# w_down of a mixture of experts loaded in longer runs of memory, with its inner index permuted

## Chip, core and metric

The kernel runs on one core of a Trainium2 chip. The metric is the device time of one execution in microseconds (us). The core has TensorE (PE, with its weight loads shown apart as PEld), VectorE (DVE), ScalarE (ACT), GpSimd (POOL), SyncE (SP, which here only issues DMAs), and 16 DMA engines that move data between HBM and SBUF.

## What is computed

One layer of a flow-matching backbone for one sample: 512 latent tokens of width 1024 and 256 context tokens. A mixer (Fourier branch, recurrent branch, merge gates, output projection) comes first; then a feed-forward part with 16 experts, in which each expert picks its 64 best tokens; then a final RMSNorm. The change lies in the experts:

```python
def expert_choice_ffn(h, w_router, w_gate, w_up, w_down):
    cap = CAPACITY_FACTOR * T // N_EXPERTS                      # 64
    scores = jax.nn.softmax(jnp.einsum('btd,de->bte', h, w_router), axis=-1)
    g, idx = lax.top_k(jnp.swapaxes(scores, 1, 2), cap)
    xg = jax.vmap(lambda hb, ib: hb[ib])(h, idx)
    hid = jax.nn.silu(jnp.einsum('becd,edf->becf', xg, w_gate)) * jnp.einsum('becd,edf->becf', xg, w_up)
    out = jnp.einsum('becf,efd->becd', hid, w_down) * g[..., None]
    return jax.vmap(lambda ib, ob: jnp.zeros((T, D), h.dtype).at[ib.reshape(-1)].add(ob.reshape(-1, D)))(idx, out)
```

All weights are float32 and each is used once. Per expert, w_gate and w_up are 1024 × 1536 and w_down is 1536 × 1024: 3 × 6.29 MB, 18.87 MB.

## The kernel before

**Stages.** The mixer takes the first part of the run. Its weights come in tiles of 1024 rows × 256 columns, so in pieces of 1 KB (`load_next`, L190 and L202); among them w_ada, whose rows are 24 KB long and of which a partition takes eight neighbouring rows, and w_in, with rows of 18 KB. Then come routing and 16 experts, then the tail: the last expert's w_down by parts of the width, and the norm.

**One expert** (the loop over `e`, up to L1216). `up_gate` multiplies the 64 gathered tokens (`xg`, in the trace `g`) with w_gate into `G`, then with w_up into `U`: eight tiles each, 32 matmuls of 384 columns each (L1111). The inner width of 1536 is held in two halves f of 768 = `FH` columns: half f lies on PSUM partitions 64 f to 64 f + 63, so `sl`, SiLU(G) × U, is 128 partitions × 768 columns. Six transposes (L1193) turn blocks of 128 of these columns into `T`, and ACT copies them (L1194) to `hT`, two tiles of three blocks, in the trace `wa` and `wd`. The w_down matmuls (L1206) take `hT` as stationary and w_down as moving operand, into `Y`; the two halves dh of the width of 1024 go to the upper and the lower 64 partitions, side by side on the array. Hooks between the tiles put in the scatter of the expert before (L1127), the ranking two experts ahead, and, in every odd expert, the gather for the next two (L1083, ahead of the transposes). On float32 a matmul leaves two records, a transpose one.

**Weight stream.** `eload` issues one tile of 768 KB per call on SP's queue: 24 units per expert in the order gate, up, down, into a ring of 22 places (rings of 14, 5 and 1 in `ew`, and `wd` and `we`). Each use of a tile is followed by one `eload`, so the stream runs about 22 tiles ahead of PE at most. Gate and up tiles (L856) are 128 whole rows of 6 KB, one per partition: one block of memory. Each DMA takes the next of eight semaphores in turn, whichever engine issues it, and before it is issued the queue waits for the DMA that used that semaphore before; so eight are under way at most.

Two small transfers on ACT's queue take places in that turn: at e = 2 `g20` is filled from `g2` (in the trace `we<-g`, L1185), and at e = 14 `g2` is copied within itself (`g<-g`, L1212). The first one stands on ACT behind the SiLU of expert 2 (L1167).

**w_down before.** A unit of experts 0 to 14 is one half dh of the width (512 columns, 2 KB) of 3 × 128 rows (L854): partition p holds rows p, p + 128 and p + 256 of them, three pieces of 2 KB. Two units, dh = 0 and 1, serve three steps of the inner width. The last expert's w_down has units of its own (`LAST`), of 512 and then 256 columns.

Of the kernel before, what the change touches and what calls it, by code (L numbers as in the profile page):

```python
# [17 lines left out]
P = 128  # L18
D = 1024
KD = D // P  # L20
# [7 lines left out]
NE = 16  # L28
CAP = 64
DE = 1536  # L30
FH = DE // 2
# [45 lines left out]
def layer(ctx: ExitStack, tc: tile.TileContext, I, out):  # L77
    nc = tc.nc
# [16 lines left out]

    # ------------------------------------------------------------------ long-lived tiles
    keep, close_keep = open_pool("keep")
# [18 lines left out]
    ident = cst[:, 0:128]  # L116
# [28 lines left out]

    # ------------------------------------------------------------------ weight stream of the mixer
    w_in, w_ada = I["w_in"][0], I["w_ada"][0]
# [151 lines left out]

    # ------------------------------------------------------------------ start: tokens, constants, adaLN of layer input  # L300
    st_p, close_st = sb("st", "right")
# [129 lines left out]

    # ------------------------------------------------------------------ constants of the recurrence
    c2, c4n, hba, hbi = (lru_c[:, i, :] for i in (4, 5, 6, 7))
# [24 lines left out]

    # ------------------------------------------------------------------ Fourier columns, as the modulation arrives
    zF = [zt("zF0"), zt("zF1")]  # L460
# [82 lines left out]

    # ------------------------------------------------------------------ 2-D DFT of the Fourier group, by its symmetries
    fT = bt.tile([P, 10, 258], F32R, tag="bt", name="fT")
# [71 lines left out]
    load_next()  # L617
    # ------------------------------------------------------------------ Fourier map to the model width
    def y4_mm(o, w, f, j, last):
# [26 lines left out]

    # ------------------------------------------------------------------ recurrent branch
    lr, close_lr = sb("lr", "right")
# [92 lines left out]

    # ------------------------------------------------------------------ merge gate A
    def zcols(w, o, c, tick=None):
# [17 lines left out]
    for i in range(4):  # L761
# [14 lines left out]
        ada_acc(J_A + i)  # L776
    # ------------------------------------------------------------------ GeLU gate times recurrence
    gp, close_gp = sb("gp", "right")
    gH = gp.tile([P, H, T], F32R, name="gH")
    gL = gp.tile([P, H, T], F32R, name="gL")  # L780
    for i in range(4):
# [10 lines left out]
        ada_acc(J_G + i)  # L792
    # ------------------------------------------------------------------ merge gate B with the recurrent map
    mH = []
# [26 lines left out]
    close_hl()  # L821
    # ------------------------------------------------------------------ expert weight stream
    NR = (14, 5, 1)
# [7 lines left out]
    EW = {}  # L831
# [3 lines left out]
    def eload():  # L835
        n = ring["n"]
        if n >= len(units):
            return
        ring["n"] += 1
        e, wn, q = units[n]  # L840
        m, i = n % (sum(NR) + 2), 0
        while i < 3 and m >= NR[i]:
            m, i = m - NR[i], i + 1
        t = rings[i].tile([P, DE], F32, tag="ew", bufs=NR[i], name=f"ew{n}") if i < 3 else held[m]
        if e == NE:
            t = t[:, 0:D]
            nc.sync.dma_start(t, flat(I["final_g"], 0, [[0, P], [1, D]]))
            EW["fg"] = t
            return
        src = I[wn][0, e]  # L850
        if wn == "w_down_e":
            c0, cw, k0, nk = q if e == NE - 1 else (512 * (q % 2), 512, 3 * (q // 2), 3)
            t = t[:, 0:cw * nk].rearrange("p (k d) -> p k d", k=nk)
            nc.sync.dma_start(t, src[P * k0:P * (k0 + nk), c0:c0 + cw].rearrange("(k p) d -> p k d", p=P))  # L854
        else:
            nc.sync.dma_start(t, src[P * q:P * q + P, :])  # L856
        EW[e, wn, q] = t

    # ------------------------------------------------------------------ output projection, residual, routing
    rt, close_rt = sb("rt", "right")  # L860
# [145 lines left out]

    # ------------------------------------------------------------------ experts
    mps, close_mps = open_pool("mps", space=PSUM)
# [146 lines left out]
    for e in range(NE):  # L1155
# [33 lines left out]
        for a in range(2):  # L1189
            t = at("T", (P, 3, P))  # L1190
            for b in range(3):
                j = 3 * a + b
                pe.transpose(t[:, b, :], sl[:, P * j:P * j + P], ident)  # L1193
            act.copy(hT[a], t)  # L1194
# [4 lines left out]
        yp = at("Y")  # L1199
        for r in range(4):  # L1200
            w = [EW.pop((e, "w_down_e", 2 * r + dh)) for dh in range(2)]
            for i in range(3):
                kf = 3 * r + i
                f, j = divmod(kf, 6)
                for dh in range(2):
                    pe.matmul(yp[64 * dh:64 * dh + 64, :], hT[j // 3][:, j % 3, 64 * f:64 * f + 64], w[dh][:, i, :],  # L1206
                              start=kf == 0, stop=kf == 11, tile_position=(0, 64 * dh))
            eload()
            eload()
# [7 lines left out]

    # ------------------------------------------------------------------ last expert by halves of the width, final norm
    ov = out[0].rearrange("(n p) d -> p n d", p=P)
# [116 lines left out]
```

## Time and profile before

| | |
|---|---|
| median of three runs | 1219.57 us (1216.5 to 1226.09) |
| span of the profiled execution | 1215.1 us |
| PE busy | 1145.7 us, 94% |
| DVE, ACT, POOL busy | 46%, 24%, 9% |
| DMA | 368.01 MB, 303 GB/s over the span |

The span runs from the first to the last instruction of one profiled execution. A page divides it into 40 slices of 30.4 us each; the digits of a slice are the busy share in tenths, and the GB/s line tells what the DMA engines moved in it. PE's busy time is not PE at its peak, since matmuls overlap. A line such as "Y<-ew,wa" names the tile written and those read.

### The profile page before, as it was taken

The page shows a single profiled execution, that of the slowest core. Times are in us where ns is not written, and L with a number is a line of the kernel's source. Part 1 is how long each engine was busy: PE and PEld are TensorE (multiplying, and loading weights), DVE is VectorE, ACT ScalarE, POOL GpSimd, SP SyncE. Part 2 cuts the span into 40 slices and gives each one's busy share as a digit, 9 for nine tenths or more (in the row PEclk, how much of TensorE's full clock was granted, in tenths as well). Part 3 has the DMA queues.
Part 4 walks back from the last instruction along what each step waited for, and adds up shares of the span by engine and source line. Part 5 has one row for each costly group of instructions (what it writes and reads, how often), then busy time and mean ns, then how long its engine had stood idle before and what let it go on. Part 6 is the DMA issues. An engine that isn't in the chain of part 4 may idle for free. (4 is left out here: it accounts for less than half of the span.)

```text
span 1215.1 us, 16698 instructions
## 1 busy us (share of the span) xinstructions
PE 1145.7 (94%) x6873; PEld 684.3 (56%) x6891; DVE 564.3 (46%) x1053; ACT 286.2 (24%) x448; POOL 112.7 (9%) x118
## 2 busy tenths in 40 slices
PE   8989988899999999999999999999999899999886
PEld 4768766688888897545445454344344344344333
DVE  5556899987666665232332342232232232232024
ACT  5543777634322222101001001001001001001004
POOL 4254343210000000000000000000000000000002
PEclk9989988999999999999999999999999999999999
DMA  8912011154664595999999999999999999999996
GB/s 310 318 62 91 21 45 53 49 183 150 207 199 148 181 395 213 314 387 416 364 408 417 403 407 418 403 408 419 409 410 418 413 413 414 410 414 411 404 399 212
DMA packets 146155, 368.01 MB, mean 303 GB/s; under 512 B 8912, under 2 KB 61656, under 8 KB 145952
## 3 DMA queue, kind: packets, MB, share of 16 engines
q1 hardware_dynamic: 143408, 363.52, 78.1%
q0 software_dynamic: 1088, 2.18, 0.6%
q10 hardware_dynamic: 1584, 1.25, 0.4%
q8 instruction: 54, 0.88, 0.3%
q14 instruction: 21, 0.17, 0.0%
HBM read 364.43 MB, written 2.10 MB: 302 GB/s over the span
## 5 line engine op out<-in xcount | busy, mean ns | idle before, releaser
L1111 PE MATMUL U<-ew,g 128*64 128x384 f32 x928 | 168.6, 495 | 10.4 <-DMA ew<-in_w_up_e 10.0
L1111 PE MATMUL G<-ew,g 128*64 128x384 f32 x960 | 174.5, 493 | 2.1 <-DMA ew<-in_w_gate_e 1.6
L1130 DVE TENSOR_TENSOR x<-x,sc 128x512 f32<-128x512 f32 x120 | 77.1, 684 | 101.9 <-PE sc L1127 101.9
L1111 PEld LDWEIGHTS U<-ew,g 128*64 128x64 f32 x928 | 59.6, 136 | 93.9 <-issue 55.0
L1111 PEld LDWEIGHTS G<-ew,g 128*64 128x64 f32 x960 | 65.7, 136 | 81.2 <-issue 60.2
L1244 POOL TENSOR_TENSOR o<-x,ew 128x512 f32<-128x512 f32 (+1 forms) x8 | 7.8, 1004 | 938.2 <-ACT o L1240 938.2
L1206 PE MATMUL Y<-ew,wd 128*64 128x512 f32 x324 | 82.8, 595 | 5.6 <-DMA ew<-in_w_down_e 5.5
L1210 DVE SCALAR_TENSOR_TENSOR wc<-Y,gc,g 128x512 f32<-128x512 f32 x15 | 11.3, 751 | 160.5 <-PE Y L1206 160.5
L1206 PE MATMUL Y<-ew,wa 128*64 128x512 f32 x312 | 78.1, 599 | 7.8 <-DMA ew<-in_w_down_e 4.6
L1194 ACT COPY wa<-T 128x384 f32<-128x384 f32 x16 | 7.7, 479 | 255.4 <-PE T L1193 255.4
L230 DVE TENSOR_TENSOR wL<-raw,wH 128x1024 fp32r<-128x1024 f32 x48 | 62.9, 1340 | 2.0 <-ACT wH L229 1.6
L1206 PEld LDWEIGHTS Y<-ew,wd 128*64 128x64 f32 x324 | 24.3, 137 | 56.5 <-issue 41.5
L1167 ACT ACTIVATE wc<-G 128x768 f32<-128x768 f32 x16 | 13.0, 811 | 178.8 <-PE G L1111 178.8
L1083 PEld LDWEIGHTS xg<-wa,xn 128*128 128x128 f32 x448 | 51.1, 192 | 0.2
L1083 PE MATMUL xg<-wa,xn 128*128 128x128 f32 x448 | 51.2, 275 | 0.0
L1206 PEld LDWEIGHTS Y<-ew,wa 128*64 128x64 f32 x312 | 23.5, 136 | 48.6 <-issue 31.7
L1049 DVE TENSOR_SCALAR wc<-wa,score 128x128 bf16<-128x128 f32 (+3 forms) x63 | 23.9, 379 | 57.0 <-ACT wa L1042 57.0
L1213 ACT CAST wb<-wc 128x512 fp32r<-128x512 f32 x15 | 9.3, 617 | 169.3 <-DVE wc L1210 169.3
L674 PE MATMUL ga<-u,gw 128*128 128x512 f32 x64 | 36.0, 645 | 10.0 <-issue 9.9
L1127 PEld LDWEIGHTS sc<-wb 64*128 64x128 f32 x240 | 23.9, 184 | 35.9 <-issue 35.3
L229 ACT CAST wH<-raw 128x1024 fp32r<-128x1024 f32 x38 | 38.0, 1045 | 18.3 <-PE zO L426 9.9
L699 POOL TENSOR_TENSOR th<-tp,th 128x768 f32<-128x768 f32 x16 | 35.0, 2205 | 49.2 <-DVE tp L698 49.2
(360 smaller groups left out, 2191.2 us busy)
## 6 DMA issues: line engine op xcount, KB each, us to landing
ew<-in_w_gate_e SPq DMA_DIRECT2D x120, 768.0 KB, 13.3
ew<-in_w_up_e SPq DMA_DIRECT2D x116, 768.0 KB, 15.0
ew<-in_w_down_e SPq DMA_DIRECT2D x113, 768.0 KB, 15.0
raw<-in_w_ada SPq DMA_DIRECT2D x24, 1024.0 KB, 5.5
raw<-in_w_in SPq DMA_DIRECT2D x16, 1024.0 KB, 4.8
wd<-in_w_down_e SPq DMA_DIRECT2D x7, 768.0 KB, 12.5
we<-in_w_down_e SPq DMA_DIRECT2D x7, 768.0 KB, 12.9
wd<-in_w_up_e SPq DMA_DIRECT2D x6, 768.0 KB, 14.6
```

The source lines that it names most:

```text
L229: (copy or act.copy)(wH[:, a], raw[:, a])
L230: dve.tensor_sub(wL[:, a], raw[:, a], wH[:, a].bitcast(F32))
L674: pe.matmul(gf[:, 512:1024], gw[:, d, i, :], u[:, TC:TA], start=True, stop=True)
L699: pool.tensor_tensor(b, s, b, op=OP.mult)
L1049: dve.tensor_scalar(GT[c][:, 0:m], sB[:, 0:m], s, None, op0=OP.is_lt)
L1083: pe.matmul(a[k // 4][:, P * (k % 4) + q.start:P * (k % 4) + q.stop], XN[n // 2][:, n % 2, P * k:P * k + P], oh[:, n, q], start=n == 0, st ...
L1111: pe.matmul(t[64 * f:64 * f + 64, n, 0:384], xg[:, k, c:c + CAP], w[:, o:o + 384], start=k == 0, stop=k == KD - 1, tile_position=(0, 64 * f))
L1127: pe.matmul(a[dh][:, c], w, v, start=j == 0, stop=j == 1, tile_position=(64 * dh, 0))
L1130: dve.tensor_add(xs, xs, a[dh])
L1167: act.activation(v3(sl), G[:, :, 0:384], AF.Silu)
L1206: pe.matmul(yp[64 * dh:64 * dh + 64, :], hT[j // 3][:, j % 3, 64 * f:64 * f + 64], w[dh][:, i, :], start=kf == 0, stop=kf == 11, tile_posi ...
L1210: dve.scalar_tensor_tensor(y, yp, gc[:, e % 3:e % 3 + 1], g2, op0=OP.mult, op1=OP.mult)
```

## The change

w_down of experts 0 to 14 is taken in pieces of 6 KB. Within each half f of the inner width, partition p now holds the six neighbouring rows 6 p to 6 p + 5, 24 KB in a row in memory; a unit is a quarter of that, 6 KB per partition, so one and a half rows of w_down. Block j of the inner width is then made of the rows 6 p + j instead of 128 j + p, and so the transposes read every sixth column of `sl`. A unit holds the whole width for one and a half blocks; the matmuls of a unit are three (j, dh) in the order of memory. The last expert keeps the sizes of its units, with the permuted rows.

```diff
         if wn == "w_down_e":
-            c0, cw, k0, nk = q if e == NE - 1 else (512 * (q % 2), 512, 3 * (q // 2), 3)
-            t = t[:, 0:cw * nk].rearrange("p (k d) -> p k d", k=nk)
-            nc.sync.dma_start(t, src[P * k0:P * (k0 + nk), c0:c0 + cw].rearrange("(k p) d -> p k d", p=P))
+            if e == NE - 1:
+                c0, cw, k0, nk = q
+                f, j = divmod(k0, 6)
+                t = t[:, 0:cw * nk].rearrange("p (k d) -> p k d", k=nk)
+                nc.sync.dma_start(t, src[FH * f:FH * f + FH, c0:c0 + cw].rearrange("(p k) d -> p k d", k=6)[:, j:j + nk])
+            else:
+                f, j = divmod(q, 4)
+                nc.sync.dma_start(t, src[FH * f:FH * f + FH, :].rearrange("(p k) d -> p (k d)", k=6)[:, DE * j:DE * j + DE])
...
                 j = 3 * a + b
-                pe.transpose(t[:, b, :], sl[:, P * j:P * j + P], ident)
+                pe.transpose(t[:, b, :], sl[:, j:FH:6], ident)
...
         yp = at("Y")
-        for r in range(4):
-            w = [EW.pop((e, "w_down_e", 2 * r + dh)) for dh in range(2)]
+        for q in range(KD):
+            w = EW.pop((e, "w_down_e", q))
+            f = q // 4
             for i in range(3):
-                kf = 3 * r + i
-                f, j = divmod(kf, 6)
-                for dh in range(2):
-                    pe.matmul(yp[64 * dh:64 * dh + 64, :], hT[j // 3][:, j % 3, 64 * f:64 * f + 64], w[dh][:, i, :],
-                              start=kf == 0, stop=kf == 11, tile_position=(0, 64 * dh))
-            eload()
+                j, dh = divmod(3 * (q % 4) + i, 2)
+                pe.matmul(yp[64 * dh:64 * dh + 64, :], hT[j // 3][:, j % 3, 64 * f:64 * f + 64], w[:, 512 * i:512 * i + 512],
+                          start=f == 0 and j == 0, stop=f == 1 and j == 5, tile_position=(0, 64 * dh))
             eload()
```

In the program of before, PE comes to the w_down matmuls of expert 0 so (the DMAHW semaphores are those of the loads, the Activation one that of the copies to `hT`):

```order
L1206 MATMUL Y<-ew_3738,wa 64x512 [waits DMAHW2_49,Activation_49]
L1206 MATMUL Y<-ew_3740,wa 64x512 [waits DMAHW3_49]
L1206 MATMUL Y<-ew_3738,wa 64x512
L1206 MATMUL Y<-ew_3740,wa 64x512
L1206 MATMUL Y<-ew_3738,wa 64x512
L1206 MATMUL Y<-ew_3740,wa 64x512
L1206 MATMUL Y<-ew_3742,wd 64x512 [waits DMAHW4_49,Activation_49]
L1206 MATMUL Y<-ew_3748,wd 64x512 [waits DMAHW5_49]
```

and in the changed program, at the same place:

```order
L1210 MATMUL Y<-ew_3738,wa 64x512 [waits DMAHW2_49,Activation_49]
L1210 MATMUL Y<-ew_3738,wa 64x512 x2
L1210 MATMUL Y<-ew_3740,wa 64x512 [waits DMAHW3_49]
L1210 MATMUL Y<-ew_3740,wa 64x512 x2
L1210 MATMUL Y<-ew_3742,wd 64x512 [waits DMAHW4_49,Activation_49]
L1210 MATMUL Y<-ew_3742,wd 64x512 x2
L1210 MATMUL Y<-ew_3748,wd 64x512 [waits DMAHW5_49]
```

The first six matmuls used two tiles in turn; now three use one tile, then three the next, and the wait for the second tile has moved two matmuls down.

On SP's queue the end of an expert's up loads and the w_down loads behind them stood so in the program of before (expert 1):

```order
L856 DMA ew_4119<-in_w_up_e 128x1536 [waits DMAHW1_49,PE_49]
L854 DMA ew_4127<-in_w_down_e 128x3x512 [waits DMAHW2_49,PE_49]
L854 DMA ew_4129<-in_w_down_e 128x3x512 [waits DMAHW3_49,PE_49]
L854 DMA wd<-in_w_down_e 128x3x512 [waits DMAHW4_49,PE_49]
L854 DMA we<-in_w_down_e 128x3x512 [waits DMAHW5_49,PE_49]
```

and in the changed one:

```order
L861 DMA ew_4119<-in_w_up_e 128x1536 [waits DMAHW1_49,PE_49]
L859 DMA ew_4124<-in_w_down_e 128x1536 [waits DMAHW2_49,PE_49]
L859 DMA ew_4129<-in_w_down_e 128x1536 [waits DMAHW3_49,PE_49]
L859 DMA wd<-in_w_down_e 128x1536 [waits DMAHW4_49,PE_49]
L859 DMA we<-in_w_down_e 128x1536 [waits DMAHW5_49,PE_49]
```

No load has moved past another and each waits on the same semaphores; only the shape of the w_down transfers is different.

## Rows read from the trace of the kernel before

**Rows 1.** The page: span, PE's busy time, GB/s by slice, DMA packets
```profile
span 1215.1 us, 16698 instructions
...
PE 1145.7 (94%) x6873; PEld 684.3 (56%) x6891; DVE 564.3 (46%) x1053; ACT 286.2 (24%) x448; POOL 112.7 (9%) x118
...
GB/s 310 318 62 91 21 45 53 49 183 150 207 199 148 181 395 213 314 387 416 364 408 417 403 407 418 403 408 419 409 410 418 413 413 414 410 414 411 404 399 212
DMA packets 146155, 368.01 MB, mean 303 GB/s; under 512 B 8912, under 2 KB 61656, under 8 KB 145952
```

**Rows 2.** Timeline of PE, first gate matmuls of experts 1, 2, 3: start, us
```profile
530.42 0.81 PE L1111 MATMUL G<-ew,g 128*64 128x384 f32 x4
...
575.59 0.81 PE L1111 MATMUL G<-ew,g 128*64 128x384 f32 x4
...
613.71 0.49 PE L1111 MATMUL G<-ew,g 128*64 128x384 f32 x2
```

**Rows 3.** PE's waits, 482 to 742, then 742 to 1153: us, times, longest
```profile
PE Y L1206 <- ACT wa L1194: 1.5, 6, 0.3
...
PE Y L1206 <- DMA ew<-in_w_down_e: 10.1, 12, 1.0
PE U L1111 <- DMA ew<-in_w_up_e: 8.5, 24, 0.4
```

**Rows 4.** Stretches with w_down alone; last three columns: PEclk, DMA share, GB/s
```profile
626.00:640.00 14.00, 13.95 (x107) 6.28 (x104) 5.64 (x16) 1.40 (x2) 0.00 (x0) 1.00 1.05 390
...
719.00:732.00 13.00, 12.71 (x117) 10.11 (x116) 3.40 (x7) 0.71 (x2) 0.00 (x0) 1.00 1.05 386
...
907.00:915.00 8.00, 7.76 (x68) 7.29 (x69) 1.44 (x4) 0.95 (x3) 0.00 (x0) 1.00 1.04 403
950.00:960.00 10.00, 9.60 (x67) 3.94 (x65) 2.99 (x6) 0.86 (x2) 0.00 (x0) 1.00 1.05 409
...
1137.00:1143.00 6.00, 4.74 (x22) 2.58 (x24) 0.31 (x1) 0.86 (x2) 0.00 (x0) 1.00 1.04 385
```

**Rows 5.** Stretches with gate and up alone; then one of the mixer's start
```profile
688.00:716.00 28.00, 28.00 (x174) 11.89 (x172) 8.26 (x18) 2.01 (x3) 0.00 (x0) 1.00 1.02 423
...
1011.00:1035.00 24.00, 24.00 (x152) 10.33 (x150) 6.70 (x13) 2.01 (x3) 0.00 (x0) 1.00 1.02 416
...
20.00:50.00 30.00, 29.06 (x207) 19.98 (x207) 13.86 (x29) 12.57 (x21) 5.24 (x4) 1.00 1.00 319
```

**Rows 6.** SP's issues around 590 us, ACT's DMA there, and SP's wait
```profile
573.21 8.41 SPq L854 DMA_DIRECT2D ew<-in_w_down_e  x6
593.00 4.00 SPq L856 DMA_DIRECT2D ew<-in_w_gate_e  x8
...
590.48 1.16 ACTq L1185 DMA_DIRECT2D we<-g  x2
...
SPq L856 <- DMA we<-g: 11.3, 1, 11.3
```

**Rows 7.** Timeline of SP: w_down issues of experts 3 and 14
```profile
613.45 16.92 SPq L854 DMA_DIRECT2D ew<-in_w_down_e  x8
...
1121.83 16.40 SPq L854 DMA_DIRECT2D ew<-in_w_down_e  x8
```

**Rows 8.** The transposes: weight loads (ns min/median/max), then one expert's in the timeline
```profile
L1193 PEld LDWEIGHTS T<-cst,wc x78: 138/140/144, 602.2 to 1137.9; 128*128 128x128 f32 x78
...
730.76 0.82 PE L1193 MATMUL T<-cst,wc 128*128 128x128 f32 x6
...
730.65 0.69 PEld L1193 LDWEIGHTS T<-cst,wc 128*128 128x128 f32 x6
```

**Rows 9.** The page's groups: busy us, mean ns | idle before
```profile
L1206 PE MATMUL Y<-ew,wd 128*64 128x512 f32 x324 | 82.8, 595 | 5.6 <-DMA ew<-in_w_down_e 5.5
```

**Rows 10.** The page's DMA issues: KB each, median us to landing
```profile
raw<-in_w_ada SPq DMA_DIRECT2D x24, 1024.0 KB, 5.5
raw<-in_w_in SPq DMA_DIRECT2D x16, 1024.0 KB, 4.8
```

## Prediction

> **What bounds the kernel now.** I read the page first, for the shape of the run. TensorE (PE) is busy for 94% of the span, but the GB/s line says more: from the 21st slice to the last but one the core takes in 399 to 419 GB/s [rows 1]. Those are the experts, whose 16 × 24 weight tiles of 768 KB (786,432 bytes) come in through SP's queue. So two things could set the time there, PE's own work or the stream, and the next views tell which.
>
> PE's timeline gives the first gate matmul of each expert. Experts 1 and 2 take 45.17 us (530.42 to 575.59, with the gather for the next two experts in it) and 38.12 us (575.59 to 613.71) [rows 2], a mean of 41.65 us. PE's waits say that these are PE's own times: up to 742 us it waits for no weight at all, only 1.5 us in total for ACT's copy of the transposes; from 742 to 1153 us it waits 10.1 us for w_down tiles and 8.5 us for w_up tiles [rows 3]. So PE uses up a stock of loaded tiles first, and after that the weights come last.
>
> The stream's pace: SP issues the first w_down tile of expert 3 at 613.45 us and that of expert 14 at 1121.83 us [rows 7]. That is eleven experts in 508.4 us, 46.22 us each, or 18.87 MB / 46.22 us = 408 GB/s. PE needs 41.65 us. From about 593 us on the stream is the bound, with 4.6 us per expert to spare on PE.
>
> Why 593 us: SP has issued expert 2's last w_down by 581.6 us and issues nothing until 593.00. The next load reuses a semaphore, and for that it waits 11.3 us for a small DMA on ACT's queue (we<-g), which ACT issues at 590.48 [rows 6]. ACT comes to it behind the SiLU of expert 2, so PE's work through expert 2's gate fixes this moment, and PE has waited for no weight by then [rows 3].
>
> **The change, part by part.** *w_down of experts 0 to 14.* A tile was 128 partitions × three pieces of 2 KB; it becomes 128 pieces of 6 KB, the form that gate and up tiles have. The bytes stay. What that is worth is read from stretches in which only one form moves. Twelve stretches, one in each w_down from expert 3 to expert 14, show 385 to 409 GB/s with the DMA share at 1.04 to 1.05, so no engine is idle in them; five of the rows stand in [rows 4]. Weighed by length, the twelve give 394.6. Eleven stretches of gate and up between them show 416 to 423 at a share of 1.02, two of them in [rows 5], weighed 419.5. A stretch early in the run, where most pieces by number have 1 KB, shows 319 at a share of 1.00 [rows 5]: the shorter the piece, the lower the rate, with the engines busy all the time. So I charge the difference to the pieces.
>
> Eight tiles are 6.29 MB: 15.94 us at 394.6, 15.00 us at 419.5, a saving of 0.94 us per expert. It counts in the twelve experts after the restart at 593 us. The w_down of experts 0 to 2 has landed or is on its way before it; there a faster transfer only makes SP's halt longer. 12 × 0.94 = 11.3 us.
>
> Bounds of this term. If w_down ran today at its best stretch (409, 15.38 us), only 0.38 us would be left per expert, 4.6 us in all. If the whole expert ran at the gate and up rate, mixed stretches too, it would take 18.87 / 419.5 = 44.99 us instead of 46.22, that is 1.23 us per expert, 14.8 us in all. I take the mean rates, 11.3.
>
> The Trainium skill prices a piece too: "DMA: Bandwidth & Descriptors", section "Why small descriptors are slow (HBM only)", gives a fixed overhead of about three bus cycles per packet beside 32 bytes per cycle. By that page's figures, an estimate, 6 KB would take 3 × (64 + 3) = 201 cycles in three pieces and 195 in one, 3% less; of 15.94 us that is 0.48 us, and 5.7 us over twelve experts. The rows show 6%, twice as much, and the sum goes by the rows.
>
> *The permuted inner index.* The transposes (six per expert) now read every sixth column of the 768. They move no other bytes, and hidden rows and w_down rows are permuted alike. No row shows a read at such a step. Today a transposed block's weight load takes 138 to 144 ns; an expert's six loads lie within 0.69 us, 0.115 us apart, its six matmuls within 0.82 us [rows 8]. The lower bound of the extra cost is nothing; as upper bound I take a read six times as slow, since six times as many bytes lie between a row's first and last element: five times 0.69 more, 3.5 us per expert. After the change the stream needs 46.22 − 0.94 = 45.28 us per expert, PE 41.65, so even 3.5 us fits under the stream, and from 593 us on the price is nothing. Ahead of 593 us there is no such cover: the transposes of experts 0 and 1 lie on PE's path to the restart. Twice as slow costs 2 × 0.69 = 1.4 us there, six times 6.9 us. I take nothing and keep 1.4 in the range.
>
> The Trainium skill speaks against this edit: "SBUF — State Buffer", section "Door 1: The DMA port swizzle", says that SBUF is read in 16-byte lines and that an access which goes to a new line each time pays a penalty; a step of 24 bytes does so each time. It gives no size for TensorE, and no run here shows one.
>
> *The w_down matmuls.* The same 24 per expert in the same order of halves, on operands of the same shape. The first now waits for one tile instead of two. PE is not the bound, so this is worth nothing, except at the end of expert 14, where PE's last w_down matmuls lead to a DMA that SP waits for again: up to one tile's three matmuls earlier. Each leaves two records, and 324 records kept PE busy for 82.8 us [rows 9], 0.26 us each, so six are 1.5 us. I leave that in the range.
>
> *SP.* It issues the same DMAs in the same order; its waits are the same. *The last expert.* Its pieces stay 2 KB and 1 KB, only their addresses move. Nothing.
>
> **Sum.** 1215.1 − 11.3 = 1203.8 us for the profiled span, which lies 4.5 us under the median of the runs, 1219.57. For the runs: 1219.57 − 11.3 = 1208.3, call it **1208**.
>
> **The rivals.**
> - *Pieces are only part of it.* A gate or up tile is one block of 768 KB in memory; the new w_down tile is 128 pieces, 24 KB apart. If half of the gap of 394.6 to 419.5 comes from the block and not from the piece, the gain is about 5.6 us: 1214. For it: no transfer in the saturated stretch has this layout. Against it: w_down's stretches change between 385 and 409 while its layout stays [rows 4], so layout is not what moves the rate most. The skill's price above would end at the same place, 1214.
> - *PE is the bound after all, and the change does not do what it says.* Then 1219, or 1221 with the transposes twice as slow. Against it: 41.65 us of work under 45.28 us of stream, and 18.6 us of waits for weights [rows 3].
> - *Slower: the 24 KB step.* If the new layout brings w_down below 394.6 GB/s, each expert loses; at 371 (16.96 us, 1.02 more than now) twelve experts lose 12.2 us, 1%. The nearest row for it: w_ada tiles, whose 1 KB pieces lie 24 KB apart, land 5.5 us after their issue at the median, w_in tiles, with 18 KB between theirs, after 4.8 [rows 10]. 0.7 us per 1024 KB would be 0.5 us per w_down tile, 96 tiles, 50 us: 1270. Against it: these loads run in the first part, where the core's rate goes from 318 down to 21 GB/s by slices [rows 1], so the queue is not full all the time and landing times tell more of what stands ahead than of the pitch.
>
> **How the numbers follow.** My forecast, w_down at the gate and up rate in a stream that stays the bound: 0.71. Pieces only in part: 0.20. PE the bound: 0.04. Slower by the step: 0.05. The forecast's own range is 1205 to 1215 (gains of 4.6 to 14.8, with 1.5 us for the end and 1.4 us for the transposes left aside). The second case reaches to 1218 or so, which I take as the upper end; the lower one is 1203, with the end of expert 14 added to the largest gain. Faster or slower by 1%, 12.2 us, is about what a measurement of this kernel can tell from no change. The forecast, 11.3, lies just inside. The mixed stretches and the end of expert 14 are on the side beyond it, the transposes and w_down's own best stretches on the near side, so I give half of the forecast's chance to more than 12.2: 0.36. Slower takes the last rival, 0.05. Within 1%: the rest, 0.59.
>
> **What would show it.** In the profile of the changed kernel: 15 × 8 × 256 = 30,720 packets fewer, about 115,400; w_down stretches at 415 to 423 GB/s instead of 385 to 409, at a DMA share near 1.02; 45.3 us between the first w_down issues of two experts; SP's halt ending again at about 593 us, and beginning about a microsecond sooner; weight loads of the transposes still at 140 ns. I am wrong if w_down's stretches stay under 410 (the piece is not the cost, or the step has one), if PE no longer waits for weights behind 742 us (PE took over), or if the halt ends clearly after 593 us (the transposes cost what they read).

## The result, and the profile after

The changed kernel takes 1206.16 us at the median of four runs (1205.51 to 1209.48), the kernel before 1218.55 us beside it; the ratio is 0.990, with an interval of 0.987 to 0.993. It is faster, by about 1%, at the bound that the prediction had set between "within 1%" and "faster". Forecast were 1208 us. Beside each other the medians lie 12.4 us apart, the spans of the two profiled executions 11.2; forecast were 11.3 for both.

The page of the changed kernel, whose lines answer to [rows 1]:

```profile
span 1203.9 us, 16716 instructions
...
PE 1148.4 (95%) x6891; PEld 684.3 (57%) x6891; DVE 564.3 (47%) x1053; ACT 286.4 (24%) x448; POOL 112.9 (9%) x118
...
GB/s 308 300 89 88 18 53 53 35 173 177 188 180 191 149 390 206 313 379 418 356 422 419 418 420 421 418 419 421 420 417 421 421 418 418 422 421 418 419 400 211
DMA packets 115435, 368.01 MB, mean 306 GB/s; under 512 B 8912, under 2 KB 61656, under 8 KB 115232
```

The span is 11.2 us shorter. The packets are 30,720 fewer, to the piece, and the GB/s line, which went up and down between 399 and 419 in the experts, now stays at 417 to 422 from the 21st slice to the 38th.

Stretches of w_down alone (four of twelve), then of gate and up alone (two of eleven); the last three columns are PEclk, DMA share and GB/s, as in [rows 4] and [rows 5]:

```profile
626.00:638.00 12.00, 12.00 (x84) 5.25 (x80) 4.40 (x13) 1.40 (x2) 0.00 (x0) 1.00 1.02 420
716.00:728.00 12.00, 12.00 (x102) 7.49 (x99) 5.31 (x15) 0.00 (x0) 0.00 (x0) 1.00 1.01 412
943.00:955.00 12.00, 11.84 (x78) 4.87 (x74) 2.99 (x6) 0.88 (x2) 0.00 (x0) 1.00 1.02 426
1125.00:1137.00 12.00, 10.65 (x48) 4.23 (x49) 0.95 (x1) 0.88 (x2) 0.00 (x0) 1.00 1.02 417
...
687.00:713.00 26.00, 25.84 (x155) 10.64 (x155) 6.22 (x12) 2.55 (x5) 0.00 (x0) 1.00 1.02 422
1003.00:1029.00 26.00, 26.00 (x162) 11.04 (x160) 7.79 (x16) 2.06 (x4) 0.00 (x0) 1.00 1.02 418
```

The twelve w_down stretches give 412 to 426 GB/s, 419.0 at the mean, against 394.6 before; gate and up are where they were (419.9 at the mean of eleven). At the mean the two forms can no longer be told apart.

Timeline of SP: the last six w_down loads of expert 2, the gate loads of expert 3, and the w_down loads of experts 3 and 14. They answer to [rows 6] and [rows 7]:

```profile
572.87 7.04 SPq L859 DMA_DIRECT2D ew<-in_w_down_e  x6
593.33 3.97 SPq L861 DMA_DIRECT2D ew<-in_w_gate_e  x8
...
613.83 13.24 SPq L859 DMA_DIRECT2D ew<-in_w_down_e  x8
...
1112.24 13.16 SPq L859 DMA_DIRECT2D ew<-in_w_down_e  x8
```

SP's wait between the first two rows (us, times, longest):

```profile
SPq L861 <- DMA we<-g: 13.4, 1, 13.4
```

From these the 11.2 us can be put in three places. The first w_down of expert 3 is issued 0.38 us later than before; 0.32 of these are there already at PE's first gate matmul of expert 0, which comes at 482.00 us before the change and at 482.32 after it. (Over all kernels here that have the small copies on ACT this moment lies between 481.17 and 482.81 us, whatever was edited behind it, so shifts of a few tenths are read from it below.) The eleven experts from there take 498.41 us instead of 508.38, 45.31 each instead of 46.22: 9.97 us less. From the first w_down of expert 14 to the end it is 91.66 us instead of 93.27: 1.61 less. From expert 0 on the two executions thus lie 11.5 us apart. The halt of SP starts 1.7 us sooner (579.9, after 581.6) and ends at almost the same time, so it has grown from 11.3 to 13.4 us.

PE's waits for weights from 742 to 1142 us, answering to the second half of [rows 3]:

```profile
PE U L1116 <- DMA ew<-in_w_up_e: 7.3, 20, 0.4
...
PE G L1116 <- DMA ew<-in_w_gate_e: 2.0, 9, 0.4
```

PE still waits for weights, but less, and in these 400 us never for w_down. The stream is still the bound.

The weight loads of the transposes (ns: minimum, median, maximum), answering to [rows 8]:

```profile
L1198 PEld LDWEIGHTS T<-cst,wc x84: 209/236/242, 602.8 to 1174.1; 128*128 128x128 f32 x84
```

The six of one expert in the timeline, and PE's first gate matmuls of experts 1, 2 and 3, answering to [rows 2]; then those of expert 0, before the change and after it:

```profile
564.63 0.96 PE L1198 MATMUL T<-cst,wc 128*128 128x128 f32 x6
...
564.52 0.88 PEld L1198 LDWEIGHTS T<-cst,wc 128*128 128x128 f32 x6
...
530.87 2.75 PE L1116 MATMUL G<-ew,g 128*64 128x384 f32 x16
...
576.11 2.75 PE L1116 MATMUL G<-ew,g 128*64 128x384 f32 x16
...
614.35 2.75 PE L1116 MATMUL G<-ew,g 128*64 128x384 f32 x16
```

```profile
482.00 1.51 PE L1111 MATMUL G<-ew,g 128*64 128x384 f32 x8
```

```profile
482.32 1.51 PE L1116 MATMUL G<-ew,g 128*64 128x384 f32 x8
```

A load of a block with the step of six takes 236 ns instead of 140. But loads overlap: the six lie within 0.88 us instead of 0.69, and an expert on PE takes 45.24 and 38.24 us instead of 45.17 and 38.12.

### The profile page after: what moved, and what is told of

It is laid out like the page before. It is cut to its first block, busy times and chain, and to the rows that moved or that the text cites. A ratio compares the mean times of both kernels' runs of the same rounds, so it can differ in the third digit from the quotient of the medians.

```text
span 1203.9 us, 16716 instructions
## 1 busy us (share of the span) xinstructions
PE 1148.4 (95%) x6891; PEld 684.3 (57%) x6891; DVE 564.3 (47%) x1053; ACT 286.4 (24%) x448; POOL 112.9 (9%) x118
## 5 line engine op out<-in xcount | busy, mean ns | idle before, releaser
L1116 PE MATMUL G<-ew,g 128*64 128x384 f32 x960 | 171.7, 493 | 3.8 <-DMA ew<-in_w_gate_e 3.5
L1116 PEld LDWEIGHTS G<-ew,g 128*64 128x64 f32 x960 | 62.8, 136 | 87.0 <-issue 62.6
L1213 DVE SCALAR_TENSOR_TENSOR wc<-Y,gc,g 128x512 f32<-128x512 f32 x15 | 11.3, 751 | 148.6 <-PE Y L1210 148.6
L1210 PE MATMUL Y<-ew,wd 128*64 128x512 f32 x324 | 77.5, 594 | 0.0
## 6 DMA issues: line engine op xcount, KB each, us to landing
we<-in_w_down_e SPq DMA_DIRECT2D x7, 768.0 KB, 12.9
```

The costliest lines, as they stand in the source:

```text
L1116: pe.matmul(t[64 * f:64 * f + 64, n, 0:384], xg[:, k, c:c + CAP], w[:, o:o + 384], start=k == 0, stop=k == KD - 1, tile_position=(0, 64 * f))
L1213: dve.scalar_tensor_tensor(y, yp, gc[:, e % 3:e % 3 + 1], g2, op0=OP.mult, op1=OP.mult)
```

## The experiments

The theory: w_down's pieces cost a fixed time each, in a stream that is the bound from the restart at 593 us on; the rest of the change is worth nothing. Rivals: the permutation or the new order of the matmuls brings the gain (waits for one tile instead of two); the pieces 24 KB apart cost part of it; the transposes take something away; PE sets the pace. Each edit is made to the changed kernel unless it says otherwise; `...` marks lines of an edit that are left out. The ratios are to the kernel before, run on the same chip.

**The permutation without the pieces.** Rows permuted and transposes strided, but units of 512 columns in pieces of 2 KB, used two at a time as before.

```diff
-                nc.sync.dma_start(t, src[FH * f:FH * f + FH, :].rearrange("(p k) d -> p (k d)", k=6)[:, DE * j:DE * j + DE])
...
+                nc.sync.dma_start(t, src[FH * f:FH * f + FH, 512 * dh:512 * dh + 512].rearrange("(p k) d -> p k d", k=6)[:, j:j + 3])
...
```

> The changed kernel with the permuted rows and the strided transposes kept, but w_down again in pieces of 2 KB: a tile is half of the width of three of a partition's six neighbouring rows, two tiles serve three steps, as before. Theory A (the stream is the bound and its rate in w_down is set by the length of the pieces): w_down at 385 to 409 GB/s again, 46.2 us per expert, a span of about 1215, ratio to before 1.00. Theory B (the rate is set by which rows lie together in a partition): w_down near 419, 45.3 us per expert, a span of about 1204, ratio 0.99.

Measured: 1218.84 us, ratio 0.999 (0.996 to 1.001). SP's w_down loads of experts 3 and 14, then a stretch of w_down alone:

```profile
613.16 18.64 SPq L861 DMA_DIRECT2D ew<-in_w_down_e  x8
...
1121.44 17.09 SPq L861 DMA_DIRECT2D ew<-in_w_down_e  x8
```

```profile
626.00:640.00 14.00, 14.00 (x108) 6.61 (x105) 5.94 (x16) 1.40 (x2) 0.00 (x0) 1.00 1.05 389
```

46.21 us per expert and 389 GB/s are the numbers of before [rows 4, 7]. The gain is in the length of the pieces, or in the order of the matmuls, which went back with it here and is taken apart below (two tiles). Permutation and strided transposes alone are worth nothing that these runs can tell, in either direction.

**One block of memory.** Pieces of 6 KB as in the change, but one tile's 128 pieces lie one behind the other (other rows of w_down).

```diff
-                nc.sync.dma_start(t, src[FH * f:FH * f + FH, :].rearrange("(p k) d -> p (k d)", k=6)[:, DE * j:DE * j + DE])
...
+                nc.sync.dma_start(t, src[192 * q:192 * q + 192, :].rearrange("r d -> (r d)").rearrange("(p c) -> p c", p=P))
```

> The changed kernel with w_down in pieces of 6 KB that follow one another in memory, so that a tile is one block of 768 KB, as a gate or up tile is; w_down's rows then don't belong to the hidden columns that they meet, so the experts' output is not the layer's, while all shapes and counts stay. Theory A (piece length): the same as the changed kernel, 45.3 us per expert, a span within 1.5 us of 1204. Rival (a step of 24 KB between pieces costs something against one block): w_down faster than its 419 GB/s of now, a span under 1202.

Measured: 1205.08 us, ratio 0.986 (0.981 to 0.992), span 1203.2, and 45.31 us per expert as in the changed kernel. Two stretches of w_down alone:

```profile
627.00:639.00 12.00, 12.00 (x95) 5.41 (x90) 4.98 (x15) 1.17 (x2) 0.00 (x0) 1.00 1.02 420
716.00:728.00 12.00, 12.00 (x104) 7.85 (x101) 5.09 (x13) 0.00 (x0) 0.00 (x0) 1.00 1.01 412
```

These are the changed kernel's 420 and 412 in the same places (to a microsecond), so the 412 is of the place and not of the layout. The rival of the 24 KB step, as part of the price or as a loss, is gone.

**Pieces of 1 KB.** The same bytes in six pieces per partition.

```diff
-                nc.sync.dma_start(t, src[FH * f:FH * f + FH, :].rearrange("(p k) d -> p (k d)", k=6)[:, DE * j:DE * j + DE])
+                nc.sync.dma_start(t.rearrange("p (k d) -> p k d", k=6),
+                                  src[FH * f:FH * f + FH, 256 * j:256 * j + 256].rearrange("(p k) d -> p k d", k=6))
```

> The changed kernel with w_down in pieces of 1 KB: a tile is a quarter of the width of six neighbouring rows; the matmuls are as in the changed kernel, so the weights meet other columns than they should and the experts' output is not the layer's. Theory A with a fixed cost per piece: 2 KB at 394.6 GB/s is 83.0 ns of one engine, 6 KB at 419.5 is 234.3 ns, so a piece costs 7.4 ns beside 37.8 ns per KB; 1 KB is 45.2 ns, 362 GB/s, w_down takes 17.4 us instead of 15.0, 2.4 us more per expert, 12 experts 28 us: a span of 1232. If short pieces cost more than in proportion, as the 319 GB/s of the mixer's start may say, up to 1260. Theory B (rows that lie together): no slower than the changed kernel. Theory C (the gain came from PE waiting for one tile instead of two): 1204.

Measured: 1240.12 us, ratio 1.016 (1.010 to 1.022), span 1235.7.

```profile
617.21 22.97 SPq L859 DMA_DIRECT2D ew<-in_w_down_e  x8
...
1141.34 22.36 SPq L859 DMA_DIRECT2D ew<-in_w_down_e  x8
```

That is 47.65 us per expert, 2.34 more than with 6 KB, where the fixed price per piece had 2.4. The 3.7 us by which the span missed 1232 have another place: the first w_down of expert 3 is issued 3.4 us later. ACT issues its small copy at 590.43 us, no later than in the changed kernel (591.00), but from 588 to 592 us the stream still moves 347 GB/s of w_down, and the copy lands after 6.3 us instead of 2.3; the restart comes at 596.79 us. The price per piece agrees over three sizes. Eight tiles take 15.00 us with 1024 pieces and 15.94 with 3072; on 16 engines that is 234 and 83 ns per piece, so 37.8 ns per KB and 7.4 ns per piece. For 1 KB this makes 45.2 ns, and 15.00 + 2.34 us over 6144 pieces is 45.2 ns.

These are means over the experts, and the price is not the same in each. The interval from expert 3's first w_down to expert 4's is 1.20 us longer in the kernel before than in the changed one, which is 9.4 ns for each of the 128 more pieces that an engine moves; with 1 KB pieces it is 3.00 us longer, 9.4 ns for each of 320. From expert 10 to expert 11 it is 0.67 us (45.61 after 44.94) and 1.49 us (46.43), 5.2 and 4.7 ns. So the two runs agree expert by expert, to about 1 ns, on a price that moves between about 4 and 9 ns; what moves it no run here shows.

**Two tiles for the first matmuls.** Pieces of 6 KB, but the matmuls go through two units at a time, so that the first ones wait for two.

```diff
-        for q in range(KD):
-            w = EW.pop((e, "w_down_e", q))
...
+        for r in range(4):
+            w = [EW.pop((e, "w_down_e", 2 * r + s)) for s in range(2)]
...
```

> The changed kernel with pieces of 6 KB, but the matmuls reordered so that the second one of six already takes the second tile, and the two loads follow the six matmuls, as before. Theory A (stream): nothing is lost, a span within 1.5 us of 1204, and PE's waits for w_down come back without any effect on the end. Theory C (the gain came from PE waiting for one tile instead of two): a good part of the 11 us is lost, 1210 to 1215.

Measured: 1206.72 us, ratio 0.989 (0.983 to 0.996), span 1203.9. PE's waits from 742 to 1142 us:

```profile
PE U L1116 <- DMA ew<-in_w_up_e: 7.2, 20, 0.4
PE Y L1210 <- DMA ew<-in_w_down_e: 5.2, 7, 0.8
```

The waits for w_down are back, 5.2 us of them, and the time is the same within the noise of the runs. That they went away in the eleven experts was no part of the gain: these take 498.46 us here and 498.41 in the changed kernel. Only at the end is something left: behind the first w_down of expert 14 it is 91.97 us after 91.66, and there SP's wait for the second small copy is 5.8 us, where it was 5.1 in the changed kernel and 6.0 before.

**Contiguous transposes.** The transposes read blocks of 128 neighbouring columns again (so rows and columns no longer belong together).

```diff
-                pe.transpose(t[:, b, :], sl[:, j:FH:6], ident)
+                pe.transpose(t[:, b, :], sl[:, P * j:P * j + P], ident)
```

> The changed kernel with the transposes on neighbouring columns again, as before, while w_down's rows stay permuted; hidden columns and rows don't belong together then, so the experts' output is not the layer's. In the changed kernel a strided weight load of a transpose took 236 ns at the median instead of 140. Theory A (the stream is the bound, only the transposes of experts 0 and 1 lie on the way to the restart): at most 0.4 us is won, a span of 1203.5 to 1204. Rival (the transposes are on the path in every expert): 16 times 0.19 us, 3 us, a span of 1201.

Measured: 1207.72 us, ratio 0.991 (0.987 to 0.994), span 1203.4. PE's first gate matmul of experts 0, 1 and 2:

```profile
481.88 1.51 PE L1116 MATMUL G<-ew,g 128*64 128x384 f32 x8
...
530.31 2.75 PE L1116 MATMUL G<-ew,g 128*64 128x384 f32 x16
...
575.48 2.75 PE L1116 MATMUL G<-ew,g 128*64 128x384 f32 x16
```

Expert 1 takes 45.17 us again, as before the change [rows 2]. The restart comes at 592.69 us, 0.64 sooner, but 0.44 of these are there at the start of expert 0 already (481.88 after 482.32). So the strided transposes cost 0.2 us on the path to the restart. From expert 0 to the end the span is 721.5 us after 721.6, and in the runs nothing can be measured.

**More work for PE, late.** Ten matmuls more ahead of the transposes in experts 3 to 14, which make an expert on PE 2.1 us longer.

```diff
+        if 3 <= e < NE - 1:
+            warm2(10)
```

> The changed kernel with ten more matmuls of 128 x 512 in bf16 ahead of the transposes of experts 3 to 14; nothing reads their result. About 0.22 us each, 2.2 us per expert, 26 us of TensorE work in all. Theory A (from the restart at 593 us on the stream is the bound with 3.6 us per expert to spare on TensorE): a span within 1.5 us of 1204, and TensorE waits less for weights. Rival (TensorE is the bound): up to 26 us more, 1230.

Measured: 1206.93 us, ratio 0.989 (0.987 to 0.992), span 1204.4, that is 0.5 us more for 25 us of work. The 0.5 us are there ahead of the work: expert 0 starts at 482.81 us, after 482.32, and from there to the end both kernels take 721.6 us. PE's waits from 742 to 1142 us:

```profile
PE U L1116 <- DMA ew<-in_w_up_e: 2.5, 3, 1.9
```

The waits for weights shrink from 9.3 us to 2.5 and the end stays. PE has its slack under the stream, and the strided transposes, which cost 0.07 to 0.12 us per expert, have some twenty times the cover they need.

**More work for PE, early.** The same ten matmuls in experts 0 and 1 alone, on PE's path to the restart.

```diff
+        if e < 2:
+            warm2(10)
```

> The same ten matmuls in experts 0 and 1 alone, 4.4 us of TensorE work. Theory A with its second half (SP's halt ends when ACT, behind expert 2's gate, issues its small copy, so TensorE's work up to there sets the restart of the stream): the restart moves from 593.3 to about 597.7 us and the end with it, a span of 1208. Rival (the stream's bytes alone set the end, the halt is hidden): 1204.

Measured: 1208.89 us, ratio 0.991 (0.988 to 0.993), span 1206.3: 2.4 us more, where 4.4 were expected. The issue of the small DMA on ACT in the changed kernel:

```profile
591.00 1.17 ACTq L1190 DMA_DIRECT2D we<-g  x2
```

and here, with SP's gate loads of expert 3 and its first w_down load behind them:

```profile
595.43 1.22 ACTq L1190 DMA_DIRECT2D we<-g  x2
...
585.45 1.93 SPq L861 DMA_DIRECT2D ew<-in_w_gate_e  x2
...
599.27 1.97 SPq L861 DMA_DIRECT2D ew<-in_w_gate_e  x4
...
615.99 13.16 SPq L859 DMA_DIRECT2D ew<-in_w_down_e  x8
```

The DMA on ACT is 4.4 us late: 4.1 by the added work and 0.3 by a later start of expert 0 (482.65 us). The restart is late even by 5.9 (599.27 after 593.33). But two gate loads went out ahead of the halt. The order of the program tells why: with other work ahead of them, the two small DMAs take other places in the turn of the semaphores. The two are the one copy into `g20`. In the changed program they stand so on ACT,

```
L1190 DMA we<-g_95 64x512 [waits DMAHW4_49]
L1190 DMA we<-g_95 64x512 [waits DMAHW6_49]
```

and in this one so:

```
L1190 DMA we<-g_95 64x512 [waits DMAHW6_49]
L1190 DMA we<-g_95 64x512 [waits DMAHW0_49]
```

SP's first gate load of expert 3 needs semaphore 4, the third needs 6. So the halt fell on the third load, and two loads at 1.87 us each (768 KB at 419.5 GB/s) passed it: 5.9 − 3.7 = 2.2 us, which is what expert 3's w_down is late (615.99 after 613.83). The path from PE over ACT to the restart is confirmed, but what a delay on it costs depends on which load shares the semaphore. That part was found after the run, not forecast.

**The halt taken away.** The two small copies, `g20` from `g2` at e = 2 and `g2` within itself at e = 14, are issued on GpSimd's queue instead of ACT's and so stand outside the turn of eight.

```diff
-                nc.scalar.dma_start(g20[64 * q:64 * q + 64, :], g2[0:64, :])
+                pool.dma_start(g20[64 * q:64 * q + 64, :], g2[0:64, :])
...
-            nc.scalar.dma_start(g2[0:64, :], g2[64:128, :])
+            pool.dma_start(g2[0:64, :], g2[64:128, :])
```

> The changed kernel with the two small copies (g2 to g20 at expert 2, within g2 at expert 14) issued from GpSimd's queue instead of ACT's, so that they take no place among the eight semaphores in turn and SP does not wait for them. In the changed kernel the stream moves 158 and 188 GB/s in the eight microseconds from 588 on and 381 and 387 in those from 1144 on; against 419 that is 4.7 and 0.7 us of stream. Theory A (stream is the bound): these come back, unless SP then waits for TensorE to free places: a span of 1198 to 1200, ratio to before 0.984 to 0.987. Rival (at that place the ring is full, so SP waits for TensorE instead): 1203.

Measured: 1200.11 us at the median of six runs, ratio 0.983 (0.981 to 0.985). This is faster than both kernels. One of the six, the profiled one, took 1214.68 us: it comes to expert 0 only at 496.63 us, and why is not known. The kernel was taken again beside its twin, the kernel before with the same two copies on GpSimd's queue:

> The changed kernel with the two small copies inside SBUF (the one that fills g20 from g2 at e = 2, the one of g2 within itself at e = 14) issued on GpSimd's queue instead of ACT's, as in the run with the copies on GpSimd ahead of this one, taken again beside its twin with w_down in 2 KB pieces. Theory (the halt at 580 to 593 us swallows what experts 0 to 2 gain): no halt at e = 2, 416 GB/s or more in every 12 us from 540 to 600, the median 6 us under the changed kernel, 1200 us, and a span near 1196 to 1199. Rival (the halt cost nothing, the six microseconds were chance): 1206.

> The kernel before (w_down in pieces of 2 KB), with only the two small copies moved to GpSimd's queue. The halt of the kernel before moved 302 GB/s over 588 to 600 us where its neighbours move 419: 1.40 MB, 3.4 us of stream, and that of the changed kernel 257 GB/s, 4.6 us. Theory (the changed kernel halts longer because its w_down of experts 0 to 2 ends sooner): without the halt this kernel gains less than the changed one does, about 3.4 us and 1 us at e = 14, so 1215; the change would then be worth 15 times 0.91 to 0.94 us, 13.7 to 14.1 us, instead of 12. Rival (the halt costs both kernels the same, and experts 0 to 2 are ahead of the bound anyway): 6 us less, 1213.5, and the change is still worth 12 us.

Measured: 1201.36 us, ratio 0.986 (0.984 to 0.987), for the changed kernel with the copies moved, and 1214.31 us, ratio 0.996 (0.994 to 0.997), for the kernel before with the copies moved. The stretch around the restart, first in the kernel before, then in the changed one, without the move:

```profile
588.00:600.00 12.00, 12.00 (x94) 5.56 (x92) 4.58 (x15) 1.40 (x2) 0.00 (x0) 1.00 0.84 302
```

```profile
588.00:600.00 12.00, 12.00 (x92) 5.43 (x89) 4.40 (x13) 1.40 (x2) 0.00 (x0) 1.00 0.70 257
```

The changed kernel with the copies moved (span 1199.8): the same stretch, PE's first gate matmul of expert 0, and SP's w_down loads of experts 3 and 14:

```profile
588.00:600.00 12.00, 12.00 (x82) 5.69 (x82) 5.68 (x15) 1.40 (x2) 0.00 (x0) 1.00 1.02 416
```

```profile
484.84 1.51 PE L1116 MATMUL G<-ew,g 128*64 128x384 f32 x8
...
611.05 12.28 SPq L859 DMA_DIRECT2D ew<-in_w_down_e  x8
...
1108.57 13.15 SPq L859 DMA_DIRECT2D ew<-in_w_down_e  x8
```

The same of the kernel before with the copies moved (span 1214.6):

```profile
588.00:600.00 12.00, 12.00 (x83) 5.48 (x81) 5.68 (x15) 1.40 (x2) 0.00 (x0) 1.00 1.03 399
```

```profile
485.59 1.51 PE L1111 MATMUL G<-ew,g 128*64 128x384 f32 x8
...
613.95 17.59 SPq L854 DMA_DIRECT2D ew<-in_w_down_e  x8
...
1122.20 16.43 SPq L854 DMA_DIRECT2D ew<-in_w_down_e  x8
```

The halt is gone in both. On GpSimd's queue nothing stands ahead of the first copy, so that it also goes out sooner, at 467.33 us in the changed kernel instead of 591.00; what standing outside the turn is worth without that was not tried. The two executions come to expert 0 at different times (484.84 and 485.59 us), so they are read from there: to the end it is 715.0 us in the one (1199.8 − 484.84) and 729.0 in the other, 14.0 us apart. Of these 2.1 us come up to the first w_down of expert 3 (126.2 us after 128.4), 10.7 in the eleven experts (497.52 after 508.25), 1.2 behind them. The profiled execution of the first run, read in the same way from 496.63 us, repeats the 126.2 and the 497.52 but has 92.5 us behind the first w_down of expert 14, where this one has 91.2: the 12.9 us up to there are seen twice, the 1.2 behind them are not. So without the halt the w_down of experts 0 to 2 counts too, which it did not in the pair with the halt, and the change is worth 12.9 to 14.0 us; the 13.7 to 14.1 that were expected lie at the upper end of that. The medians of the runs lie 12.95 us apart, between the two forecasts of 12 and 13.7, and do not decide; on the side of before this rests on one profiled execution.

All three traces with the copies moved come to expert 0 later than the nine others (484.84 us and more, after 482.81 at most), so the move may cost something there; that was not tried.

## Why the prediction was right

**The bound and its pace.** Right. The stream sets the end from the restart on, both with the work of PE made longer (late) and with its waits changed (two tiles). 45.3 us per expert were forecast, 45.31 came.

**The main term.** 0.94 us for each of twelve experts were forecast. Measured were 0.91 per expert over eleven, 9.97 us. The assumption behind it, that the difference of 394.6 and 419.5 GB/s belongs to the pieces and to all of the difference, is what the first three experiments show: with 2 KB pieces the rate and the pace of before, with 6 KB in one block or 24 KB apart the same, with 1 KB the price per piece that the other two sizes give. The term's upper bound, mixed stretches included (14.8 us), was not reached. The mean hides that the saving goes from 1.20 us in expert 3 to 0.52 in expert 9: that one mean rate for all of w_down served is good fortune in part. With expert 14 the term is 10.9 us, 0.4 under the 11.3; that the span comes within 0.1 of the sum, 11.2, is due to the 0.7 us at the end, which were only in the range. The forecast lay just inside the bound of 1% and had its larger chance there, 0.59; the measured 0.990 lies just on the other side, which had 0.36, and its interval holds both.

The Trainium skill's price, three bus cycles per packet ("DMA: Bandwidth & Descriptors", section "Why small descriptors are slow (HBM only)"), would have given 5.7 us in all, by the estimate from that page's figures. The runs say about twice that, so of the two readings weighed against each other in the prediction the rows were the better one. That each piece costs something beside its bytes, the page has right; that this is always the same, these runs do not bear out (about 9 ns in expert 3, 5 in expert 10).

**The strided transposes.** The sum was right, the sentence on the weight loads wrong. "Weight loads of the transposes still at 140 ns" was forecast, 236 ns came. The step of it that failed is the value between the two bounds: no row showed a read at such a step, and nothing was taken. What saved the sum is that a load runs beside the one before it, so that 96 ns more per load become 0.19 us per six, and 0.07 to 0.12 us per expert on PE. On the path to the restart that is 0.2 us: from the start of expert 0 ACT comes to its small copy after 108.68 us, after 108.48 before the change and 108.49 with contiguous transposes. It is within the 1.4 us that had been kept. (That the halt ends at 593.33 after 593.00 is not this: expert 0 starts 0.32 later.) The rule which the prediction held against this edit, a penalty for an access that goes to a new line each time ("SBUF — State Buffer", section "Door 1: The DMA port swizzle", of the Trainium skill), agrees with these loads in its direction; the run with contiguous transposes gives its worth, those 0.2 us.

**The halt.** Forecast was an end at about 593 us and a start about a microsecond sooner. It ends at 593.33 and starts 1.7 us sooner, and so the gain of the w_down ahead of it is lost, as forecast. The runs without the halt show the same from the other side: 2.1 us come back there. One thing the prediction left out: between the SiLU of expert 2 and the small copy ACT has one more instruction, a copy for the ranking that waits 1.00 us for PE, so PE fixes the restart a little behind expert 2's gate.

**The w_down matmuls.** Nothing was forecast, with up to 1.5 us for the end of expert 14. The two-tile run has the span of the changed kernel to a tenth of a microsecond, but its expert 0 starts 0.47 us sooner, and 0.3 of these are lost behind the first w_down of expert 14, with SP's second wait for a small copy 0.7 longer. So the term is some 0.3 us by these two executions, within the 1.5, and close to what single executions scatter. The 1.61 us behind the first w_down of expert 14 are that expert's share of the main term, 0.9, perhaps these 0.3, and 0.4 more, whose cause was not tried.

**The rivals.** "Pieces are only part of it" fell with the single block, at 1205.08 us. "PE is the bound after all" fell with 25 us of added work that cost nothing from expert 0 on. "Slower by the 24 KB step" fell with both: 419.0 GB/s with the step, 420 and 412 without, in the places where the changed kernel has 420 and 412.

## What to carry to other kernels

Where loads set the pace, compare the rates of stretches in which one form of transfer moves: the gap between them, times the bytes, forecast this change to about a microsecond, and it needed no price from elsewhere. Count only the loads behind the last point at which the stream stands still for another reason; what is gained ahead of it goes into a longer halt. Then look for what ends that halt: here two small copies on another engine's queue shared semaphores with the weight stream, and moving them brought 5 to 6 us more than the longer pieces alone (1201.36 and 1200.11 us after 1206.16). And count shifts of a few tenths of a microsecond from a point ahead of the edit, since two executions do not reach it at the same time.

## What the runs showed of the hardware that was not expected

- A weight load of a 128 × 128 float32 block read with a step of six elements takes 236 ns instead of 140, but six in a row only 0.88 us instead of 0.69.
- In the full stream a transfer of many pieces holds the queue that issues it. SP's issue of a w_down tile, in ns (minimum, median, maximum), with three pieces per partition and then with one:

```profile
L854 SPq DMA_DIRECT2D ew<-in_w_down_e x115: 367/1684/4227, 468.8 to 1192.6; - x115
```

```profile
L859 SPq DMA_DIRECT2D ew<-in_w_down_e x106: 327/328/616, 469.2 to 1125.1; - x106
```

- The price of a piece moved along the run, alike for pieces of 1 KB and of 2 KB: 9.4 ns more per piece in expert 3, about 5 in expert 10. The cause is open.
- Added work on PE ahead of a small DMA moved that DMA's place in the turn of the semaphores, and with it the load that the halt fell on; 5.9 us of delay became 2.2.
